# Expert weights dealt to partitions in 8 KB runs, with the down product, the fetch depth and two small pieces rearranged to match

## The chip, the core and the metric

The kernel runs on one core of a Trainium2 chip. The metric is device time in microseconds (us), from the start to the end of one execution, and the number compared is the median over executions.

The engines are named as the profile names them: PE (TensorE, matmuls; PEld is its loading of the stationary operand), ACT (ScalarE), DVE (VectorE), POOL (GpSimd) and SP (SyncE, which issues nearly all weight loads). "SPq L114" and the like is an engine's instruction queue rather than its arithmetic.

## What is computed

Two post-norm layers over 512 tokens of width 1024. Layer 0 mixes the tokens with a state-space model and a pooling branch, layer 1 with stick-breaking attention. After each mixer comes the same feed-forward stage, and only that stage is touched by the change:

```python
for i in range(DEPTH):                       # DEPTH = 2
    ...                                      # the mixer, out projection, layer norm
    ple = (p[i] @ ple_w_proj[i]) * jax.nn.sigmoid(x @ ple_w_gate[i])
    ffn = grouped_moe(x, router_w, router_bias, moe_w1[i], moe_w3[i], moe_w2[i])
    x = layer_norm(DEEPNORM_ALPHA * x + ffn + ple, ...)

def grouped_moe(x, router_w, router_bias, w1, w3, w2):
    ...                                      # sigmoid scores, best group of 4, top 2 experts in it, gates
    h = jax.nn.silu(jnp.einsum('td,edf->etf', xt, w1)) * jnp.einsum('td,edf->etf', xt, w3)
    h = h * gates.T[:, :, None]
    y = jnp.einsum('etf,efd->td', h, w2)
```

There are 16 experts. `w1` and `w3` are 1024 x 512 per expert, `w2` is 512 x 1024, all in fp32, so one expert is 6 MB and one layer's experts are 96 MB.

## The kernel before

`ffn(layer)` writes x to DRAM, routes, and ranks the experts by their number of tokens. It then works through the experts in the order of the table SEQ, which holds ranks: 1, 2, 11, 3, 4, 12, 5, 6, 13, 7, 14, 8, 15, 9, 16, 10. An expert of rank 1 to 10 gets room for 96 tokens (CAP), one of rank 11 to 16 for 64 (SMALL). Tokens beyond that room go through `overflow` (L1141, L1222), an If on all engines that stands behind expert 12 of the order; here it is not entered, but its branch is executed.

For an expert e of the order:

- `gather(e)` (L1015, POOL) fetches its tokens from DRAM into `xg`. `load_g(e)` transposes them on PE (L1042) into a PSUM bank `pT`, from which ACT and DVE make `g`: for a CAP expert a high part on ACT (L87) and a remainder on DVE (L88), for a SMALL one a plain copy.
- `up(e, kh, a)` multiplies `g` with `w1` (a = 0) and `w3` (a = 1), 512 rows (kh) at a time, into the banks `pA`. For CAP each fp32 product is three matmuls (`mm3`, L92 to L94) of high parts and remainders, so the weights too are split: ACT writes `w_..h` (L87), DVE `w_..l` (L88), 1024 columns of a raw tile at a time. For SMALL the raw tile is multiplied directly in fp32 (L1072), two column halves side by side.
- `act(e)` applies silu on ACT (`sg`, L1079 or L1082) and the product on DVE. `turn(e)` transposes `sg` on PE (L1091) and makes `sT`.
- `down(e)` multiplies `sT` with `w2` into the banks `pB` (CAP: `mm3`; SMALL: L1115), ACT evicts to `ysb` (L1139), and `scatter(e)` (L1022, POOL) sends the rows to `yd` in DRAM.

The loop over e interleaves two experts: silu of e, first half of up of e + 1, turn of e, rest of that half, down of e, then `load_g(e + 2)` and the second half of up of e + 1. Behind expert 13 of the order, `last_onehot` (L1198) builds the one-hot matrix of the last expert (`ohl`, 16 small matmuls at L1209 and L1211, evicted by ACT to `oht` and `gs`), so that the last expert's output need not go through DRAM. Behind expert 15 the final sum is made from the reloaded `yd` (`yt`, L1156) and `oht`; one quarter of the gate product (`pG`) and the layer norm follow.

Weights arrive in loads of 1 MB, issued on SP at L114 from a queue planned in advance (`plan_ffn`); six of them belong to an expert. `weights(LA)` and `plain(LA)` take the next raw tile and issue loads up to LA further in the queue. The raw tiles share 17 slots of 8 KB per partition with x, `g`, `xg`, `oht` and others, so a load also waits for a slot. The split halves go through rings of 5 (`wh`) and 6 (`wl`) tiles of 1024 columns. Each engine runs its instructions in the order in which they stand; that order was fixed when the program was built, by a scheduler that models the engines.

The lines that the change touches are the weight load's source view, the operand slices of the transposes, `down`, and the place of `last_onehot`:

```python
src = ap.rearrange("(k p) n -> p k n" if len(ap.shape) == 2 else "o (k p) n -> p (o k) n", p=128)
...
nc.tensor.transpose(p[:, k * c:(k + 1) * c], xgs[:c, e % 2, kb * 128:(kb + 1) * 128],
```

With `(k p)`, a partition of a raw tile holds four separate rows of 512 columns, 2 KB each in DRAM.

## Time and profile before

| | |
|---|---|
| median of 3 executions | 1253.8 us (1252.96 to 1254.33) |
| the profiled execution, its own time | 1255.37 us |
| span of its trace | 1253.7 us |
| PE busy | 1138.2 us (91%) |
| DVE, ACT, POOL busy | 63%, 47%, 10% |
| mean granted TensorE clock | 0.96 |

The profiled execution took 1.57 us more than the median, and its trace leaves 1.67 us of it outside the span; positions below are counted from the span's start. The experts of layer 0 run from about 255 to 549 us, those of layer 1 from about 905 to 1215 us. The page's strip of DMA activity is full in just these stretches; PE is busy nine tenths and more in most of their slices too.

### The profile page before, as it was taken

The numbers are of one execution on the slowest core, as the hardware profiler recorded it, in microseconds if no ns is written. First come the engines' busy times: TensorE is split into PE (matmuls) and PEld (weight loads), VectorE is DVE, ScalarE is ACT, GpSimd is POOL, SyncE is SP. The second block draws the span as 40 slices with busy tenths as digits, with TensorE's granted clock in tenths as the row PEclk, the third lists the DMA queues.
The fourth block names the chain that finished last, engine by engine and source line by source line (L and its number), as shares of the span: only waits on it lengthen the run. The fifth ranks groups of instructions, "written<-read, shape, count | busy, mean of one in ns | idle before, by whom it ended". The sixth has DMA issues, their size and how long they took to land. (4 is left out here: it accounts for less than half of the span.)

```text
span 1253.7 us, 16680 instructions
## 1 busy us (share of the span) xinstructions
PE 1138.2 (91%) x6191; PEld 795.7 (63%) x6191; DVE 790.1 (63%) x1252; ACT 594.4 (47%) x895; POOL 127.8 (10%) x150
## 2 busy tenths in 40 slices
PE   5986998999899887999999999998999899997885
PEld 3866788756457443477867767688865467553454
DVE  5998766866465443486477467756877465443465
ACT  4322542656465443454465456523476465444451
POOL 5010020111010110001000000011101110100001
PEclk9997999999899997999999999998999899988888
DMA  8225563599998996973112024434299999998861
GB/s 248 68 69 189 196 230 114 163 369 375 377 368 298 370 375 245 329 272 101 34 47 89 1 68 151 154 142 153 76 365 370 372 368 322 365 364 291 279 261 67
DMA packets 157391, 285.05 MB, mean 227 GB/s; under 512 B 18816, under 2 KB 42896, under 8 KB 156240
## 3 DMA queue, kind: packets, MB, share of 16 engines
q1 hardware_dynamic: 143760, 256.56, 58.0%
q0 software_dynamic: 8800, 25.19, 6.2%
q10 hardware_dynamic: 4736, 2.10, 0.6%
q8 instruction: 52, 0.85, 0.3%
q14 instruction: 43, 0.35, 0.1%
HBM read 270.45 MB, written 18.61 MB: 231 GB/s over the span
## 5 line engine op out<-in xcount | busy, mean ns | idle before, releaser
L88 DVE TENSOR_TENSOR w_0l<-raw,w_0h 128x1024 fp32r<-128x1024 f32 (+1 forms) x161 | 192.2, 1194 | 72.9 <-ACT w_0h L87 72.1
L87 ACT ACTIVATE w_0h<-raw 128x1024 fp32r<-128x1024 f32 (+1 forms) x161 | 166.4, 1033 | 74.2 <-DMA raw<-in_moe_w_dram 34.7
L88 DVE TENSOR_TENSOR w_2l<-raw,w_2h 128x1024 fp32r<-128x1024 f32 x133 | 162.0, 1218 | 39.8 <-ACT w_2h L87 39.8
L87 ACT ACTIVATE w_2h<-raw 128x1024 fp32r<-128x1024 f32 x133 | 139.7, 1051 | 30.9 <-PE pA L94 28.7
L92 PE MATMUL pA<-w_0h,g 128*96 128x512 f32 x160 | 71.1, 444 | 32.5 <-ACT g L87 28.0
L1072 PE MATMUL pA<-raw,g 128*64 128x512 f32 x384 | 99.6, 621 | 0.0
L1139 ACT ACTIVATE ysb<-pB 96x512 f32<-96x512 f32 (+1 forms) x60 | 35.7, 594 | 97.7 <-PE pB L1115 56.3
L1015 POOL DMA_INDIRECT xg<-xd,ixm x32 | 35.1, 1098 | 363.9 <-PE pT L1042 295.4
L94 PE MATMUL pA<-w_0h,g 128*96 128x512 f32 x160 | 68.0, 425 | 2.1 <-DVE g L88 2.0
L93 PE MATMUL pA<-w_0l,g 128*96 128x512 f32 x160 | 67.9, 424 | 2.2 <-DVE w_0l L88 2.2
L92 PE MATMUL pA<-w_2h,g 128*96 128x512 f32 x160 | 65.9, 412 | 0.0
L93 PE MATMUL pA<-w_2l,g 128*96 128x512 f32 x160 | 65.5, 410 | 0.0
L94 PE MATMUL pA<-w_2h,g 128*96 128x512 f32 x160 | 65.2, 408 | 0.0
L92 PEld LDWEIGHTS pA<-w_0h,g 128*96 128x96 f32 x160 | 27.9, 174 | 56.6 <-ACT g L87 35.1
L1022 POOL DMA_INDIRECT yd<-ysb,ixm x30 | 34.2, 1140 | 241.6 <-ACT ysb L1139 236.7
L1072 PEld LDWEIGHTS pA<-raw,g 128*64 128x64 f32 x384 | 26.1, 139 | 44.1 <-issue 40.1
L692 DVE TENSOR_TENSOR_SCAN kw<-kw 128x128 f32<-128x128 f32 (+3 forms) x64 | 50.2, 812 | 0.9 <-ACT kw L689 0.6
L1115 PE MATMUL pB<-raw,sT 128*64 128x512 f32 x192 | 46.0, 599 | 0.0
L1080 DVE TENSOR_TENSOR sg<-sg,pA 96x512 f32<-96x512 f32 x20 | 13.6, 682 | 47.3 <-PE pA L94 36.6
L1042 PEld LDWEIGHTS pT<-ident,xg 96*128 96x128 f32 (+1 forms) x256 | 22.4, 142 | 28.9 <-issue 20.0
L1042 PE MATMUL pT<-ident,xg 96*128 96x96 f32 (+1 forms) x256 | 26.5, 244 | 15.3 <-DVEq L1222 7.8
L88 DVE TENSOR_TENSOR w_4l<-raw,w_4h 128x1024 fp32r<-128x1024 f32 x20 | 24.4, 1221 | 24.6 <-ACT w_4h L87 24.3
(467 smaller groups left out, 2812.7 us busy)
## 6 DMA issues: line engine op xcount, KB each, us to landing
raw<-in_moe_w_dram SPq DMA_DIRECT2D x192, 1024.0 KB, 11.6
raw<-in_sb_w_qkv_dram SPq DMA_DIRECT2D x12, 1024.0 KB, 5.1
raw<-in_ple_w_gate_dram SPq DMA_DIRECT2D x8, 1024.0 KB, 5.0
yt<-yd SPq DMA_DIRECT2D x8, 1024.0 KB, 8.9
raw<-in_ab_w_out_dram SPq DMA_DIRECT2D x4, 1024.0 KB, 7.7
xd<-x0r POOLq DMA_DIRECT2D x8, 512.0 KB, 4.1
raw<-in_sb_w_out_dram SPq DMA_DIRECT2D x4, 1024.0 KB, 5.4
raw<-in_ab_w_in_dram SPq DMA_DIRECT2D x3, 1024.0 KB
```

The costliest lines, as they stand in the source:

```text
L87: return (self.nc.scalar.activation(hi, src, AF.Copy), (self.nc.gpsimd if pool else self.nc.vector).tensor_tensor(lo, src, hi.bitcast(F32) ...
L88: (self.nc.gpsimd if pool else self.nc.vector).tensor_tensor(lo, src, hi.bitcast(F32), op=OP.subtract))
L92: t.matmul(out, s[0], m[0], start=first, stop=False)
L93: t.matmul(out, s[0], m[1], start=False, stop=False)
L94: t.matmul(out, s[1], m[0], start=False, stop=last)
L692: v.tensor_tensor_scan(rv, rv, rv, 1.0, op0=OP.mult, op1=OP.min)
L1015: return nc.gpsimd.indirect_dma_start(out=xgs[:c, e % 2, :], out_offset=None, in_=xd[:, :], in_offset=bass.IndirectOffsetOnAxis(ap=self.ix ...
L1022: nc.gpsimd.indirect_dma_start(out=yd[:, :], out_offset=bass.IndirectOffsetOnAxis(ap=self.iy[:c, r:r + 1], axis=0), in_=src[:c], in_offset ...
L1042: nc.tensor.transpose(p[:, k * c:(k + 1) * c], xgs[:c, e % 2, kb * 128:(kb + 1) * 128], self.ident[:c, :c])
L1072: nc.tensor.matmul(hh[0][x * 64:x * 64 + 64], g[:, kb], self.pair[x][:, k], start=(kb == 0), stop=(kb == KB - 1))
L1115: nc.tensor.matmul(py[x * 64:x * 64 + 64], sT[:, k], w[x][:, k], start=(k == 0), stop=(k == 3))
L1139: nc.scalar.activation(ysb[:rows(e), h], py, AF.Copy)
```

## The change

Five edits, all in the feed-forward stage or its constants.

1. The expert weights are dealt to partitions by `(p k)` instead of `(k p)`: partition p holds k consecutive rows, one run of 8 KB in DRAM. `w2` is planned as two pieces of 256 rows x 1024 columns instead of two of 512 rows x 512 columns, so that its runs are 8 KB too. The other operand must be dealt in the same way, so the transposes of `xg` read every fourth column of the stationary operand and those of `sg` every second.
2. `down` follows: for CAP both `pB` banks are open at once, one weight piece feeds both column halves, and the two evictions come together at the end. For SMALL the first raw tile is used up before the second.
3. The fetch depth LA stays 6 to the end of the experts instead of falling to 3 at expert 13; a limit keeps the queue from running on into the next layer's weights until the `yt` loads are issued.
4. `last_onehot` stands behind `load_g(e + 2)` instead of ahead of it, and writes its result into the unused end of the last `g` tile instead of a raw slot of its own.
5. The rank constant `kb` is made by GpSimd (an iota and two memsets) instead of three DVE operations.

```diff
     def prefetch(self, upto, parts=1):
-        while self.loaded < min(upto, len(self.queue)):
-            ap, k, n = self.queue[self.loaded]
+        while self.loaded < min(upto, self.limit or len(self.queue)):
+            ap, k, n, rows = self.queue[self.loaded]
...
-            src = ap.rearrange("(k p) n -> p k n" if len(ap.shape) == 2 else "o (k p) n -> p (o k) n", p=128)
+            o = "" if len(ap.shape) == 2 else "o "
+            src = ap.rearrange(f"{o}(p k) n -> p ({o}k) n" if rows else f"{o}(k p) n -> p ({o}k) n", p=128)
...
-        nc.vector.tensor_copy(self.kb, self.w16)
+        nc.gpsimd.iota(self.kb, pattern=[[-1, 16]], base=16, channel_multiplier=0,
+                       allow_small_or_imprecise_dtypes=True)
         for e in range(2):
-            nc.vector.tensor_scalar(self.kb[:, e:e + 1], self.kb[:, e:e + 1], float((2 - e) << 15), None, op0=OP.add)
+            nc.gpsimd.memset(self.kb[:, e:e + 1], float(((2 - e) << 15) + 16 - e))
...
-                    kb = hf * 4 + k
-                    nc.tensor.transpose(p[:, k * c:(k + 1) * c], xgs[:c, e % 2, kb * 128:(kb + 1) * 128],
+                    nc.tensor.transpose(p[:, k * c:(k + 1) * c], xgs[:c, e % 2, hf * 512 + k:(hf + 1) * 512:4],
...
-                nc.tensor.transpose(p[:, k * c:(k + 1) * c], sg[:, k * 128:(k + 1) * 128], self.ident[:c, :c])
+                a = k // 2 * 256
+                nc.tensor.transpose(p[:, k * c:(k + 1) * c], sg[:, a + k % 2:a + 256:2], self.ident[:c, :c])
...
             if rows(e) == CAP:
-                for h in hs:
+                py = [self.bank("B", "pB")[:CAP] for _ in hs]
+                for a in range(2):
                     w = self.weights(LA)
-                    py = self.bank("B", "pB")[:CAP]
-                    for k in range(4):
-                        self.mm3(py, (sT[:, 0, k], sT[:, 1, k]), w[k], k == 0, k == 3)
-                    yield h, py
-                return
-            w = [self.plain(LA), self.plain(LA)]
...
+                    for q in range(2):
+                        k = 2 * a + q
+                        for x, h in enumerate(hs):
+                            self.mm3(py[x], (sT[:, 0, k], sT[:, 1, k]), [t[:, h] for t in w[q]], k == 0, k == 3)
...
+            yield from zip(hs, py)
+
+        self.limit = self.ends[layer]
...
-            LA = 6 if e < 13 else 3
...
-            if e == NE - 3:
-                oht = self.last_onehot()
-                self.ln_setup("ln_ffn", layer)
...
             if e + 2 < NE:
                 gn = load_g(e + 2)
+            if e == NE - 3:
+                oht = self.last_onehot(self.gtile[:, 2 * KB * CAP:])
+                self.ln_setup("ln_ffn", layer)
...
+        self.limit = None
+        LA = 3
...
-                self.plan(part(e, n, slice(kh * 512, (kh + 1) * 512)), 4, 512)
+                self.plan(part(e, n, slice(kh * 512, (kh + 1) * 512)), 4, 512, True)
...
-                self.plan(part(e, "moe_w2", slice(None), slice(nh * 512, (nh + 1) * 512)), 4, 512)
+                self.plan(part(e, "moe_w2", slice(nh * 256, (nh + 1) * 256)), 2, 1024, True)
...
+        self.ends[layer] = len(self.queue)
```

The program is scheduled anew, so instructions also move where the diff shows nothing. Three places matter. The line numbers of the changed kernel are a few higher (L87 is L89 there, L92 to L94 are L94 to L96, L1072 is L1076, L1139 is L1147); `raw_1722` and the like are raw tiles by number, and `w_0h` and `w_2h` (or `w_1h`) are the two halves of one raw tile after ACT's split.

The first place is ACT around the end of the first CAP expert's down product in layer 0. Before:

```order
L87 ACTIVATE w_0h<-raw_1722 128x1024
L87 ACTIVATE w_2h<-raw_1722 128x1024
L1139 ACTIVATE ysb<-pB 96x512
L87 ACTIVATE w_0h<-raw_2150 128x1024
L87 ACTIVATE w_2h<-raw_2150 128x1024
L1139 ACTIVATE ysb<-pB 96x512
L1051 ACTIVATE g_2_2284<-pT 128x256
```

and after the change:

```order
L89 ACTIVATE w_0h<-raw_1722 128x1024
L89 ACTIVATE w_2h<-raw_1722 128x1024
L89 ACTIVATE w_0h<-raw_2150 128x1024
L89 ACTIVATE w_2h<-raw_2150 128x1024
L1147 ACTIVATE ysb<-pB 96x512 x2
L1055 ACTIVATE g_2_2284<-pT 128x256
```

The first eviction has moved behind the two splits for the next expert, and both now stand together. What follows them is the same.

The second place is ACT near the end of layer 0's experts, from the evictions of expert 13 of the order on (`g_15` belongs to the last expert, a CAP one; `sg` with 64 rows and `ysb` with 64 rows to expert 14, a SMALL one). Before:

```order
L1139 ACTIVATE ysb<-pB 96x512 x2
L1213 ACTIVATE oht<-pT 128x512
L1215 ACTIVATE gs<-pT 128x1
L87 ACTIVATE g_15_4584<-pT 128x384 x2
L87 ACTIVATE w_0h<-raw_4521 128x1024
L87 ACTIVATE w_2h<-raw_4521 128x1024
L1082 ACT_TABLE_LOAD
L1082 ACTIVATE sg<-pA 64x512
L87 ACTIVATE w_0h<-raw_4599 128x1024
L87 ACTIVATE w_2h<-raw_4599 128x1024
L1139 ACTIVATE ysb<-pB 64x512 x2
L87 ACTIVATE w_0h<-raw_4645 128x1024
```

and after the change:

```order
L1147 ACTIVATE ysb<-pB 96x512 x2
L89 ACTIVATE w_0h<-raw_4482 128x1024
L1086 ACT_TABLE_LOAD
L1086 ACTIVATE sg<-pA 64x512
L89 ACTIVATE w_2h<-raw_4482 128x1024
L89 ACTIVATE w_0h<-raw_4484 128x1024
L89 ACTIVATE w_2h<-raw_4484 128x1024
L89 ACTIVATE g_15_4554<-pT 128x384 x2
L1222 ACTIVATE g_15_4554<-pT 128x512
L1224 ACTIVATE gs<-pT 128x1
L89 ACTIVATE w_0h<-raw_4604 128x1024
L89 ACTIVATE w_2h<-raw_4604 128x1024
```

The last expert's `g_15` has moved behind the silu of expert 14 and three weight splits. The splits of its second half of w1 and w3 (`raw_4604` here, `raw_4645` before) have moved ahead of the evictions of expert 14.

The third place is PE at the same point, where `ohl` is the one-hot matrix of `last_onehot`. Before, from the end of expert 13's down product:

```order
L94 MATMUL pB<-w_2h,sT 96x512
L1209 MATMUL pT<-ident,ohl 128x128 x8
L1211 MATMUL pT<-gates_1776,ohl 128x1 x8
L1072 MATMUL pA<-raw_4431,g_14_4418 64x512
L1042 MATMUL pT<-ident,xg_1500 128x96 x8
L1072 MATMUL pA<-raw_4453,g_14_4418 64x512
```

and after the change, from the end of expert 14's second up half:

```order
L1076 MATMUL pA<-raw_4431,g_14_4418 64x512
L1076 MATMUL pA<-raw_4453,g_14_4418 64x512
L94 MATMUL pA<-w_0h,g_15_4554 96x512
L95 MATMUL pA<-w_0l,g_15_4554 96x512
L94 MATMUL pA<-w_0h,g_15_4554 96x512
L1219 MATMUL pT<-ident,ohl 128x128 x8
L1221 MATMUL pT<-gates_1776,ohl 128x1 x8
L96 MATMUL pA<-w_0h,g_15_4554 96x512
```

The one-hot matmuls have moved behind expert 14's up product and behind the first three matmuls of expert 15. Further on, six matmuls of the gate (`pG`) now stand between the transposes of expert 15's `sg` and the rest of its down product, where before the whole of `pG` came behind it.

## Rows read from the trace of the kernel before

**Rows 1.** The page's first part: busy time, share of the span, instructions.
```profile
PE 1138.2 (91%) x6191; PEld 795.7 (63%) x6191; DVE 790.1 (63%) x1252; ACT 594.4 (47%) x895; POOL 127.8 (10%) x150
```

**Rows 2.** Windows: length; busy PE, PEld, DVE, ACT, POOL; clock; DMA share; GB/s.
```profile
255.00:485.00 230.00, 214.48 (x1014) 125.81 (x1013) 126.49 (x137) 119.40 (x154) 27.23 (x24) 0.96 1.01 360
885.00:1190.00 305.00, 282.26 (x1383) 173.25 (x1382) 174.77 (x228) 160.04 (x202) 35.99 (x33) 0.96 0.92 324
265.00:270.00 5.00, 5.00 (x21) 2.70 (x21) 1.78 (x2) 1.68 (x3) 0.00 (x0) 1.00 1.05 388
540.00:545.00 5.00, 3.86 (x13) 2.32 (x14) 4.65 (x6) 3.81 (x8) 0.00 (x0) 0.75 1.01 424
1205.00:1210.00 5.00, 3.58 (x17) 1.92 (x15) 4.10 (x4) 3.94 (x6) 0.00 (x0) 1.00 1.03 431
```

**Rows 3.** The page's DMA issues: count, KB each, median us to landing.
```profile
raw<-in_moe_w_dram SPq DMA_DIRECT2D x192, 1024.0 KB, 11.6
```

**Rows 4.** What PE waited for, 230 to 560 us: total us, times, longest.
```profile
PE pA L92 <- ACT g L87: 14.0, 5, 5.0
PE pT L1042 <- DVEq L1222: 3.7, 1, 3.7
PE pT L1042 <- PEq L1222: 2.5, 1, 2.5
PE pA L92 <- ACT w_0h L87: 2.2, 1, 2.2
```

**Rows 5.** What ACT waited for in the same stretch, the row on loads.
```profile
ACT w_0h L87 <- DMA raw<-in_moe_w_dram: 15.0, 8, 4.3
```

**Rows 6.** ACT's timeline: start, length, instruction, idle before and releaser.
```profile
325.77 0.59 ACT L1082 ACTIVATE sg<-pA 64x512 f32<-64x512 f32 x1 [3.69 <-PE pA L1072]
326.38 1.06 ACT L87 ACTIVATE w_0h<-raw 128x1024 fp32r<-128x1024 f32 x1
...
330.18 0.85 ACT L87 ACTIVATE g<-pT 128x384 fp32r<-128x384 f32 x2
```

**Rows 7.** PE's timeline at the same place.
```profile
330.70 0.62 PE L92 MATMUL pA<-w_0h,g 128*96 128x512 f32 x1 [5.01 <-ACT g L87]
...
336.69 0.63 PE L94 MATMUL pA<-w_2h,g 128*96 128x512 f32 x1
```

**Rows 8.** ACT's timeline near the end of layer 0's experts.
```profile
518.28 0.59 ACT L1082 ACTIVATE sg<-pA 64x512 f32<-64x512 f32 x1
...
529.17 1.20 ACT L1139 ACTIVATE ysb<-pB 64x512 f32<-64x512 f32 x2 [8.26 <-PE pB L1115]
```

**Rows 9.** PE's timeline there, experts 13 to 15 of the order.
```profile
501.56 1.94 PE L1072 MATMUL pA<-raw,g 128*64 128x512 f32 x8
503.43 0.47 PE L92 MATMUL pB<-w_0h,sT 128*96 128x512 f32 x1
...
509.06 1.95 PE L1209 MATMUL pT<-ident,ohl 128*128 128x128 f32 x16
...
512.62 1.07 PE L1072 MATMUL pA<-raw,g 128*64 128x512 f32 x2
...
531.36 0.47 PE L92 MATMUL pA<-w_0h,g 128*96 128x512 f32 x1 [2.23 <-ACT w_0h L87]
532.62 0.74 PE L93 MATMUL pA<-w_0l,g 128*96 128x512 f32 x1 [0.79 <-DVE w_0l L88]
...
540.35 0.55 PE L1091 MATMUL pT<-ident,sg 96*128 96x96 f32 x4 [0.78 <-DVE sg L1080]
541.48 0.47 PE L92 MATMUL pB<-w_0h,sT 128*96 128x512 f32 x1 [0.58 <-ACT sT L87]
...
549.09 0.28 PE L92 MATMUL pG<-w_0h,cath 128*128 128x256 f32 x1
```

**Rows 10.** Stationary loads by line: ns min/median/max, first and last start, form.
```profile
L286 PEld LDWEIGHTS pT<-ident,s5in x16: 183/202/205, 25.1 to 29.8; 64*128 64x128 f32 x16
L181 PEld LDWEIGHTS pT<-ident,x x32: 180/230/231, 7.7 to 24.5; 128*128 128x128 f32 x32
```

More of the change, by code (lines that the diff above doesn't have):

```diff
@@ L55, in __init__ @@
         self.cat = None
+        self.limit = None
+        self.ends = {}
         self.order = {}
@@ L94, in mm3, with plan @@
         t.matmul(out, s[1], m[0], start=False, stop=last)
-    def plan(self, ap, k, n):
-        self.queue.append((ap, k, n))
+    def plan(self, ap, k, n, rows=False):
+        self.queue.append((ap, k, n, rows))
         return len(self.queue) - 1
     def prefetch(self, upto, parts=1):
-        while self.loaded < min(upto, len(self.queue)):
-            ap, k, n = self.queue[self.loaded]
+        while self.loaded < min(upto, self.limit or len(self.queue)):
+            ap, k, n, rows = self.queue[self.loaded]
             if callable(ap):
@@ L121, in weights @@
         self.used += 1
-        ap, k, n = self.queue[i]
+        _, k, n, _ = self.queue[i]
         raw = self.raws.pop(i)
@@ L490, in plain @@
         self.used += 1
-        ap, k, n = self.queue[i]
+        _, k, n, _ = self.queue[i]
         return self.raws.pop(i)[:, :k * n].rearrange("p (k n) -> p k n", k=k)
@@ L1034, in load_g @@
             if c == CAP:
-                g = self.slot(f"g{layer}_{e}", F32R)[:, :2 * KB * c].rearrange("p (a k t) -> p a k t", a=2, k=KB)
+                self.gtile = self.slot(f"g{layer}_{e}", F32R)
+                g = self.gtile[:, :2 * KB * c].rearrange("p (a k t) -> p a k t", a=2, k=KB)
             else:
@@ L1157, in ffn @@
             yts.append(yt)
+        self.limit = None
+        LA = 3
         yl = self.slot(f"yl{layer}", F32R).rearrange("p (a d) -> p a d", a=2)
@@ L1196, in ffn, with last_onehot @@
             pass
-    def last_onehot(self):
+    def last_onehot(self, oht):
         nc, v = self.nc, self.nc.vector
@@ L1211, in last_onehot @@
             nc.tensor.matmul(pg[:, 0:1], oh[:, x], self.gates[:, x % 2, x // 2], start=(x == 0), stop=(x == 2 * NT - 1))
-        oht = self.slot("oht", F32R)[:, :512]
         nc.scalar.activation(oht, p, AF.Copy)
```

15 lines of the change are left out of this document (9 added, 6 removed).

## The prediction

> **What bounds the kernel now.** I read the page's busy shares first, then the windows over the two expert stretches, then what PE waited for in them, and last the timelines around the longest waits. PE is busy 91% of the span [rows 1]. In the expert stretches it is busy 214.5 us of 230 and 282.3 of 305, while the DMA engines are busy all of the time or nearly so (shares of 1.01 and 0.92) [rows 2]. So two resources look full, and the first question is which of them holds the end. The waits answer it: in layer 0's expert stage PE waits 14.0 us for `g` from ACT, 6.2 us at the overflow branch and 2.2 us for a split weight [rows 4]; no row of that list names a transfer of expert weights as what PE waited for. ACT does wait for weight loads, 15.0 us in 8 places [rows 5], but PE isn't held there, since the splits run ahead of it. So PE, with the order in which ACT serves it, is the bound, and DMA is a close second with little to spare.
>
> What PE's longest wait looks like: ACT sits idle until a SMALL expert's up product is done, then runs silu (0.59 us), four weight splits and only then the `g` that PE needs; from 326.38 to 330.18 are four splits, 0.95 us each [rows 6]. PE waits 5.01 us there, and its next 13 CAP matmuls (330.70 to 336.69, a short second wait among them) take 5.99 us where 13 at the pace of expert 13's down product, 24 in 5.63 us or 0.235 each [rows 7, 9], would take 3.05. Without the second wait (about half a us) that is some 2.4 us lost to a lower granted clock after the wait. That it is the clock I take from the window 540 to 545, just behind two shorter waits: its mean granted clock is 0.75, while those without a wait ahead of them show 1.00 [rows 2]. A wait of several us therefore costs about half as much again.
>
> **The change part by part.**
>
> *8 KB runs.* The same 192 loads of 1 MB [rows 3] move the same bytes. In stretches where weight loads alone run, with 2 KB pieces, 388 GB/s were reached; in those where the `yt` loads with their 8 KB rows ran in the queue 424 and 431 [rows 2]. 1.049 MB take 2.70 us at 388 GB/s and 2.45 at the mean of the latter two, 0.25 us less; for 192 loads 48 us of DMA time. Little of it is on the path: where ACT waits less for a load, it then waits longer for PE. I take 0; the bounds are 0 and the rival below.
>
> *Strided operands of the transposes.* The same number of transposes, with a stationary operand read at a stride of 16 or 8 bytes. The nearest row is L286, which reads every sixteenth fp32 column: 183 to 205 ns a load; L181 in the same early stage, unit stride, takes 180 to 231 [rows 10]. The shapes differ (64 partitions against 128), and stride shows no price. I take 0, with the rival below as upper end.
> The Trainium skill speaks against it: "SBUF — State Buffer", in Door 1: The DMA port swizzle, states that SBUF has 16-byte lines, needs two hits on a line for full bandwidth and lets an access that crosses to a new one pay. By it the stride of 16 bytes here would pay at each element, as should the one of 64 bytes in L286; the trace does not agree [rows 10]. By the row the sum has nothing for this edit; by the rule it would have the price of the last rival.
>
> *The new down.* The matmul count is the same. In the ACT order one eviction moves behind two splits. That lets ACT split the next expert's weights up to half a down product (2.8 us) sooner, but what PE waits for next is `g` or `sT` behind the same instructions as before, so I take 0. The scatter starts up to 0.6 us later, and nobody on PE waits for it.
>
> *Fetch depth, and `last_onehot`.* They act only behind expert 13, where the order is a different one. Layer 0, from PE's rows [rows 9] and ACT's [rows 8]:
> - Removed: PE waits 2.23 us for the first split of expert 15's second half, which stood behind an eviction that waited 8.26 us for PE; it now stands ahead. From there to the wait before 540.35 the 24 matmuls take 540.35 - 0.78 - 531.36 = 8.21 us against 5.63: 2.58 more, of which 0.79 is a second wait and the rest the lower clock. The wait of 0.58 for `sT` is filled with six gate matmuls. The down product then takes 549.09 - 541.48 = 7.61 us against 5.63, 1.98 more. Together 2.23 + 2.58 + 0.58 + 1.98 = 7.4 us.
> - Added: `g_15` now stands behind expert 14's silu and three splits. ACT can start that silu only when PE ends expert 14's up product; with the one-hot matmuls (512.62 - 509.06 = 3.56 us) moved behind, that is near 513.4. The table load ahead of the silu fits into ACT's idle time. Then 0.59 + 3 x 0.95 + 0.43 (half of the 0.85 for `g`) = 3.9 us, so PE waits about 4.0 us, as in [rows 7], and loses about 2.4 us of clock after it. The one-hot matmuls, now behind three of expert 15's, also need both `pT` banks back from `g`'s remainder on DVE: about 0.5 us. Together 6.9 us.
> - Between them stands an amount that I can't place. The stretch is 549.09 - 509.06 = 40.0 us long. In it are 72 CAP matmuls (16.9 us), the one-hot ones (3.6), 32 records of SMALL products (four times the 1.87 us that eight take from 501.56), sixteen transposes (about 2.2, from the four of 0.55 at 540.35), waits of 2.23 + 0.79 + 0.78 + 0.58 = 4.4 and clock losses of 1.8 + 2.0: 38.4 in all. The other 1.6 us lie where single SMALL products stand among other work, an estimate. The new order has them in groups of four and eight, so part of it goes.
>
> Net of the tail: between 7.4 - 6.9 = 0.5 us and 0.5 + 1.6 + 2.4 = 4.5 us saved, the latter if the clock doesn't fall after the new wait. At the other end, if the lower clock in the down product stays (the wait of 0.78 for `sg` is still ahead of it) and the wait for `g_15` is 5.0 as in [rows 7]: 0.5 - 2.0 - 1.0 = -2.5, a loss. I take 2.0 us saved in each layer, between the first two, since most of what is removed stands in rows and the dearer form of the new wait doesn't. Layer 1 has the same order. That `oht` no longer takes a slot only matters to loads that PE doesn't wait for.
>
> *Rank constant.* Three DVE operations at the start become three on POOL, which is busy a tenth of the span [rows 1]; nothing of the experts starts before the router needs it. 0. If POOL were late there, it would be by the length of such an operation, below what can be seen.
>
> *The rest.* The overflow branch keeps its 6.2 us per layer: they are waits for the sequencers, which the change doesn't touch. The long waits for `g`, 14.0 us per layer, stay too: their order on ACT (silu, two or four splits, then `g`) is the same.
>
> Sum: the profiled execution's 1255.4 us less 2 x 2.0 = 4.0 us gives 1251.4; that execution stands 1.6 above the median. On the median's scale 1253.8 - 4.0 = **1249.8 us**.
>
> **The rivals.**
>
> *DMA was the bound after all.* For it: shares of 1.01 and 0.92, ACT's 15.0 us of waiting for loads [rows 2, 5]. Then faster loads would shorten the experts until PE is full. PE's free time in the two stretches is 15.5 + 22.7 = 38.2 us [rows 2], less than the 48 us of DMA time, so it would be 1253.8 - 38.2 = 1215.6, about 1216. Against it: nothing in [rows 4] names a load, and the largest of those waits begin with ACT waiting for PE [rows 6].
>
> *Nothing measurable.* The tail's new wait eats what the old ones gave (0.5 us saved per layer, the lower end above), or the scheduler's new order does nothing elsewhere: 1253.8 - 1.0 = 1252.8.
>
> *Slower, through `g_15`.* In the tail PE waits for `g_15` behind expert 14's silu and three splits. With 5.0 us of wait, the clock loss behind it, and the down product still at the lower clock, each layer loses 2.5 us, so 1253.8 + 5.0 = 1258.8. It decides from the point where the new wait with its clock exceeds 7.4 us. For it: three waits of this very form stand in the experts and cost 14.0 us per layer with shorter ones [rows 4]. Against it: here are three splits, not four.
>
> *Slower, through the strides.* Each of the 384 transposes would take the length of a load such as those of [rows 10], some 0.2 us, once more, if PE can't hide it: 384 x 0.2 = 77 us, 1331. The same rows speak against it.
> By the cited rule of the Trainium skill's SBUF page it would be this case.
>
> **How the numbers follow.** Chances: the forecast (1244.8 to 1252.3) 0.53, DMA bound 0.13, nothing 0.15, slower through `g_15` 0.17, strides 0.02. A change of 0.2%, 2.5 us, is about what a measurement of this kernel can tell from none. Of the forecast's 0.53 some 0.1 lies within that, so faster is 0.43 + 0.13 = 0.56, within 0.1 + 0.15 = 0.25, slower 0.17 + 0.02 = 0.19. The range takes in the tail's bounds on the slow side (1253.8 + 5.0, rounded up to 1260). On the fast side it goes to 1226, some way towards the DMA rival, because part of ACT's waits for loads could turn out to reach PE. Left out are most of that rival and the strides, and a little above 1260, together under 0.2.
>
> **What would show it.** Right: weight loads land sooner and the DMA share in the expert stretches falls to about 0.9; the waits for `g` at the three places of [rows 4] are unchanged; the wait of 2.2 us for `w_0h` near the end of the experts is gone, and one of about 4 us for `g` stands some 15 us earlier; the transposes' stationary loads keep their mean. Wrong: PE's waits for `g` in mid stage shrink, the loads of L1042's successor take longer, or the expert stage as a whole is shorter by ten us or more, which would mean that ACT's waits for loads did reach PE.

## The result, and the profile after the change

The changed kernel takes 1267.3 us (median of 4 executions, 1262.87 to 1272.53), the kernel before 1253.6 (4 executions): a ratio of 1.011 with a 95% interval of 1.006 to 1.016. It is slower by 13.7 us where 4 us less were forecast, and outside the forecast range. The profiled execution took 1270.5 us, with a span of 1268.7.

The page looks almost the same. Its first part, which answers to [rows 1]:

```profile
PE 1155.3 (91%) x6191; PEld 819.9 (65%) x6191; DVE 790.2 (62%) x1249; ACT 595.3 (47%) x895; POOL 129.7 (10%) x153
```

PE has the same 6191 matmuls and is busy 17.1 us longer: PE itself does its work more slowly. The DMA side got what it was meant to get. The windows of the changed kernel (columns as in [rows 2]) and its DMA issues:

```profile
255.00:490.00 235.00, 218.74 (x1002) 131.15 (x1002) 125.25 (x136) 117.66 (x150) 27.75 (x24) 0.96 0.91 348
265.00:270.00 5.00, 5.00 (x22) 2.97 (x20) 2.77 (x3) 1.73 (x2) 0.00 (x0) 1.00 1.01 419
```

```profile
raw<-in_moe_w_dram SPq DMA_DIRECT2D x192, 1024.0 KB, 8.3
```

In the same five microseconds 419 GB/s where there were 388, a DMA share of 0.91 in the expert stretch where there was 1.01, and 8.3 us from issue to landing instead of 11.6 [rows 3]. And the kernel is slower.

To see where, I took the start of PE's first transpose of `xg` for each expert, of its down products and of the final sum from the two traces, and set the stretches between them side by side (us, from the profiled executions; experts of the order are counted from 0, so expert 13 is the last but two, and the third expert is number 2):

| stretch on PE | before | after | difference |
|---|---|---|---|
| start to the first expert, layer 0 | 228.8 | 225.2 | -3.6 |
| first to third expert | 26.6 | 28.7 | +2.1 |
| third expert to expert 13 of the order | 205.9 | 213.0 | +7.1 |
| to expert 13's down product (branch in it) | 42.1 | 41.8 | -0.3 |
| to expert 15's down product | 38.1 | 42.7 | +4.6 |
| to the final sum | 14.8 | 12.7 | -2.1 |
| to the first expert of layer 1 | 339.5 | 340.0 | +0.5 |
| first to third expert, layer 1 | 26.5 | 27.3 | +0.8 |
| third expert to expert 13 | 206.5 | 213.4 | +6.9 |
| to expert 13's down product (branch in it) | 40.9 | 37.1 | -3.8 |
| to expert 15's down product | 39.3 | 42.5 | +3.2 |
| to the final sum, and to the end | 44.7 | 44.3 | -0.4 |

Four things stand in it: mid stage is 7 us longer in each layer, the tail some 2.5 us (4.6 less 2.1, and 3.2 less 0.4), and two stretches are shorter in places that the prediction passed over, the start and the branch of layer 1.

**Mid stage.** The groups of stationary loads, one line per shape (busy us, mean ns of one, then idle time before them), of the kernel before:

```profile
L1042 PEld LDWEIGHTS pT<-ident,xg 96*128 96x128 f32 x160 | 15.0, 141 | 9.8 <-issue 6.4 <-ACT gs L1215 1.6
L1091 PEld LDWEIGHTS pT<-ident,sg 96*128 96x128 f32 x80 | 8.1, 144 | 14.6 <-DVE g L1049 4.9 <-issue 4.7 <-DVE sg L1080 4.1
```

and of the changed kernel, where L1046 and L1096 are the same transposes with strided columns:

```profile
L1046 PEld LDWEIGHTS pT<-ident,xg 96*128 96x128 f32 x160 | 22.3, 216 | 8.1 <-issue 6.5
L1096 PEld LDWEIGHTS pT<-ident,sg 96*128 96x128 f32 x80 | 11.6, 212 | 14.3 <-DVE g L1053 4.9 <-issue 4.5 <-DVE sg L1084 4.3
```

Each load takes some 70 ns longer, with a stride of two columns as with one of four. There are 384 of them, so some 27 us more of loading; the transposes' own matmul records grew from 43.3 us in all to 59.1. That is most of PE's 17 us.

**The tail.** PE's timeline of the changed kernel, experts 14 and 15 of layer 0:

```profile
523.02 0.47 PE L94 MATMUL pA<-w_0h,g 128*96 128x512 f32 x1 [4.06 <-ACT g L89]
...
524.96 3.75 PE L1219 MATMUL pT<-ident,ohl 128*128 128x128 f32 x16 [0.82 <-DVE g L90]
528.50 3.41 PE L1221 MATMUL pT<-gates,ohl 128*128 128x1 f32 x16
531.78 0.72 PE L96 MATMUL pA<-w_0h,g 128*96 128x512 f32 x1
...
536.94 0.60 PE L95 MATMUL pA<-w_0l,g 128*96 128x512 f32 x1
```

The wait for the last `g` is there with 4.06 us (4.0 were forecast). What was not forecast is what the one-hot matmuls cost behind it: they take 531.78 - 524.96 = 6.8 us where they took 3.56 [rows 9]. The window over them shows why:

```profile
525.00:537.00 12.00, 12.00 (x47) 9.98 (x47) 0.28 (x1) 3.40 (x5) 0.00 (x0) 0.50 0.86 338
```

The granted clock is 0.50, the lower of the two levels (1.2 GHz), for all of these twelve microseconds, in which PE is never idle; in the window behind, 537 to 549, it is 0.99.

**The start.** DVE's and PE's timeline of the kernel before:

```profile
12.67 0.17 DVE L167 COPY kb<-w 128x16 f32<-128x16 f32 x1 [7.08 <-POOL w L164]
...
13.01 0.21 DVE L247 COPY s5sm<-pT 128x64 f32<-128x64 f32 x1
```

```profile
13.51 1.11 PE L181 MATMUL pT<-ident,x 128*128 128x128 f32 x4 [4.64 <-ACT s5sm L248]
```

DVE's copy of the rank constant waited 7.08 us for GpSimd's iota, and everything behind it on DVE's queue waited with it, up to a PSUM bank that PE needed. In the changed kernel the copy of `s5sm` stands at 5.63 us and PE goes on at 9.51 with a wait of 0.78:

```profile
5.63 0.17 DVE L251 COPY s5sm<-pT 128x64 f32<-128x64 f32 x1
```

```profile
9.51 1.97 PE L185 MATMUL pT<-ident,x 128*128 128x128 f32 x8 [0.78 <-ACT s5sm L252]
```

**The branch.** PE's waits over the whole run, the rows for DVE's overflow branch, first of before, then of after:

```profile
PE pT L1042 <- DVEq L1222: 7.8, 2, 4.2
```

```profile
PE pT L1046 <- DVEq L1231: 2.9, 1, 2.9
```

In layer 1 the wait is gone.

### The profile page after: what moved, and what is told of

It is laid out like the page before. It is cut to its first block, busy times and chain, and to the rows that moved or that the text cites. A ratio compares the mean times of both kernels' runs of the same rounds, so it can differ in the third digit from the quotient of the medians.

```text
span 1268.7 us, 16688 instructions
## 1 busy us (share of the span) xinstructions
PE 1155.3 (91%) x6191; PEld 819.9 (65%) x6191; DVE 790.2 (62%) x1249; ACT 595.3 (47%) x895; POOL 129.7 (10%) x153
## 5 line engine op out<-in xcount | busy, mean ns | idle before, releaser
L89 ACT ACTIVATE w_0h<-raw 128x1024 fp32r<-128x1024 f32 (+1 forms) x161 | 166.4, 1033 | 49.7 <-PE pG L96 27.2
L90 DVE TENSOR_TENSOR w_2l<-raw,w_2h 128x1024 fp32r<-128x1024 f32 x93 | 113.4, 1220 | 47.7 <-ACT w_2h L89 47.6
L89 ACT ACTIVATE w_2h<-raw 128x1024 fp32r<-128x1024 f32 x93 | 97.9, 1053 | 48.2 <-PE pA L96 40.7
L94 PE MATMUL pA<-w_0h,g 128*96 128x512 f32 x160 | 71.5, 447 | 35.4 <-ACT g L89 35.4
L1076 PE MATMUL pA<-raw,g 128*64 128x512 f32 x384 | 97.3, 620 | 0.0
L1147 ACT ACTIVATE ysb<-pB 96x512 f32<-96x512 f32 (+1 forms) x60 | 35.3, 591 | 105.2 <-PE pB L1124 58.8
L96 PE MATMUL pA<-w_0h,g 128*96 128x512 f32 x160 | 68.3, 427 | 2.0 <-DVE g L90 1.9
L94 PEld LDWEIGHTS pA<-w_0h,g 128*96 128x96 f32 x160 | 28.3, 177 | 59.1 <-ACT g L89 44.3
L94 PE MATMUL pA<-w_2h,g 128*96 128x512 f32 x160 | 65.9, 412 | 0.0
L96 PE MATMUL pA<-w_2h,g 128*96 128x512 f32 x160 | 65.3, 408 | 0.0
L1076 PEld LDWEIGHTS pA<-raw,g 128*64 128x64 f32 x384 | 25.8, 139 | 43.5 <-issue 39.9
L90 DVE TENSOR_TENSOR w_1l<-raw,w_1h 128x1024 fp32r<-128x1024 f32 x40 | 48.8, 1219 | 3.6 <-ACT w_1h L89 3.2
L1046 PEld LDWEIGHTS pT<-ident,xg 96*128 96x128 f32 (+1 forms) x256 | 34.8, 215 | 22.5 <-issue 15.0
L89 ACT ACTIVATE w_1h<-raw 128x1024 fp32r<-128x1024 f32 x40 | 42.0, 1051 | 10.6 <-PE pA L96 10.6
L1046 PE MATMUL pT<-ident,xg 96*128 96x96 f32 (+1 forms) x256 | 37.0, 285 | 10.7 <-PEq L1231 5.0
L1084 DVE TENSOR_TENSOR sg<-sg,pA 96x512 f32<-96x512 f32 x20 | 13.6, 682 | 48.6 <-PE pA L96 48.6
```

Source lines behind the costliest of these rows:

```text
L89: return (self.nc.scalar.activation(hi, src, AF.Copy), (self.nc.gpsimd if pool else self.nc.vector).tensor_tensor(lo, src, hi.bitcast(F32) ...
L90: (self.nc.gpsimd if pool else self.nc.vector).tensor_tensor(lo, src, hi.bitcast(F32), op=OP.subtract))
L94: t.matmul(out, s[0], m[0], start=first, stop=False)
L96: t.matmul(out, s[1], m[0], start=False, stop=last)
L1076: nc.tensor.matmul(hh[0][x * 64:x * 64 + 64], g[:, kb], self.pair[x][:, k], start=(kb == 0), stop=(kb == KB - 1))
L1084: v.tensor_tensor(sg, sg, hh[1][:CAP], op=OP.mult)
```

## The experiments

Theories: S, the strided loads are the main cost; T, the new tail; D, something on the DMA side. Later ones are named where they come up. Medians stand beside the kernel before measured in the same session, with the ratio's 95% interval.

**e1: the changed kernel with unit-stride reads.** PE, ACT and SP have the same instructions in the same order as in the changed kernel.

```diff
-                    nc.tensor.transpose(p[:, k * c:(k + 1) * c], xgs[:c, e % 2, hf * 512 + k:(hf + 1) * 512:4],
+                    nc.tensor.transpose(p[:, k * c:(k + 1) * c], xgs[:c, e % 2, hf * 512 + k * 128:hf * 512 + (k + 1) * 128],
...
-                nc.tensor.transpose(p[:, k * c:(k + 1) * c], sg[:, a + k % 2:a + 256:2], self.ident[:c, :c])
+                nc.tensor.transpose(p[:, k * c:(k + 1) * c], sg[:, k * 128:(k + 1) * 128], self.ident[:c, :c])
```

> The changed kernel with the transposes of xg and sg reading unit-stride columns again; the instruction order is the same on every engine. Which features meet which weight rows is then wrong: this leaves out the dealing of the other operand, the work is the same. Theory S (the strided stationary loads cost time on PE: 213 ns a load in the changed kernel against 142 before, PE busy 59.1 us on the 384 transposes against 43.3): some 14 to 16 us less than the changed kernel, about 1252, and loads of about 142 ns. Theory D (the strides are hidden and something of the larger DMA runs or the tail holds the kernel): no change, about 1267. Theory T (the tail's new order is the main cost): still about 1262 or more.

1252.9 us (10 executions), before 1253.4, ratio 1.000 (0.999 to 1.001). So the strides are worth 14.5 us, as theory S had it, and without them the change would be a draw. The changed kernel's four executions lie up to 10 us apart, so a difference from it is known to some 6 us only; e2 and e3 give the strides' price again. The draw is itself a sum, as the next runs show.

**e2: the kernel before with strided reads alone.**

```diff
-                    nc.tensor.transpose(p[:, k * c:(k + 1) * c], xgs[:c, e % 2, kb * 128:(kb + 1) * 128],
+                    nc.tensor.transpose(p[:, k * c:(k + 1) * c], xgs[:c, e % 2, hf * 512 + k:(hf + 1) * 512:4],
...
-                nc.tensor.transpose(p[:, k * c:(k + 1) * c], sg[:, k * 128:(k + 1) * 128], self.ident[:c, :c])
+                nc.tensor.transpose(p[:, k * c:(k + 1) * c], sg[:, k // 2 * 256 + k % 2:k // 2 * 256 + 256:2], self.ident[:c, :c])
```

> The kernel before, with strided reads in the transposes alone (every fourth column of xg, every second of sg); the order is the same as before on every engine, weights as before, so the dealing of features to rows is wrong. Theory S: about 1253.6 + 14 = 1268. Theory D and T: about 1254, since nothing else moved.

1273.0 us against 1253.4, ratio 1.016 (1.014 to 1.019): 19.5 us for the strides here. A third pair is e3 and e6 below, which differ in the strides alone: 1267.1 less 1250.8, 16.3 us. The spread of the changed kernel's executions covers the difference between the three.

**e3: the changed kernel with the old tail**, edits 3 and 4 undone.

```diff
-        self.limit = self.ends[layer]
...
+            LA = 6 if e < 13 else 3
...
+            if e == NE - 3:
+                oht = self.last_onehot(self.slot("oht", F32R)[:, :512])
+                self.ln_setup("ln_ffn", layer)
             if e in GATES:
                 gate(GATES.index(e))
...
-            if e == NE - 3:
-                oht = self.last_onehot(self.gtile[:, 2 * KB * CAP:])
-                self.ln_setup("ln_ffn", layer)
```

> The changed kernel with the fetch depth and the place and slot of the last one-hot as before (edits 3 and 4 undone). The last g then stands ahead of the silu on ACT again. Theory T: the wait of 4 us for the last g with the slow one-hot matmuls behind it goes, 3 to 5 us a layer, about 1258 to 1261. Theory S with a neutral tail: 1266 to 1268.

1267.1 us, where the changed kernel has 1267.3: theory T gets nothing from this pair, though the spread of the changed kernel's executions could hide a few us.

**e4: the kernel before with the new tail alone**, the same edits the other way round.

> The kernel before with edits 3 and 4 alone (fetch depth, place and slot of the last one-hot). Theory T: 3 to 5 us a layer slower, about 1260. Theory S with a neutral tail: 1252 to 1255.

1259.3 us against 1253.4, ratio 1.005 (1.003 to 1.007), 5.8 us slower. Its tail reads like that of the changed kernel: a wait of 4.07 us for the last `g`, then the one-hot matmuls from 519.15, the next group of them at 522.69. So T holds on the old kernel, and whether it holds on the new one e3 alone can't tell; e6 and e13 below say more.

**e5: the kernel before with the rank constant on GpSimd**, edit 5 alone.

```diff
-        nc.vector.tensor_copy(self.kb, self.w16)
+        nc.gpsimd.iota(self.kb, pattern=[[-1, 16]], base=16, channel_multiplier=0,
+                       allow_small_or_imprecise_dtypes=True)
         for e in range(2):
-            nc.vector.tensor_scalar(self.kb[:, e:e + 1], self.kb[:, e:e + 1], float((2 - e) << 15), None, op0=OP.add)
+            nc.gpsimd.memset(self.kb[:, e:e + 1], float(((2 - e) << 15) + 16 - e))
```

> The kernel before with edit 5 alone (rank constant on GpSimd). Theory K: in the trace of before DVE stands 7.08 us at the copy of the rank constant, waiting for GpSimd's iota, with work behind it for which PE waits 4.6 us; that goes, 4 to 5 us. The same edit takes three instructions off DVE's program; the wait for DVE's branch in layer 1, 4.2 us, is absent in the three runs that have this edit and present in the three that don't, so it may go too: 1245 to 1249. The view of my prediction (a constant that nothing waits for): 1253.

1244.0 us against 1252.9, ratio 0.993 (0.991 to 0.995). The smallest edit is worth 8.9 us, more than was expected of it, and alone it beats both kernels. Its trace has the first expert at 225.0 us instead of 228.8, and the branch row of layer 1 is gone:

```profile
PE pT L1043 <- DVEq L1223: 3.1, 1, 3.1
```

**e6: the changed kernel with unit reads and the old tail.** What is left of the change is the 8 KB runs, the new down product and the rank constant (the edits of e1 and e3 together).

> The changed kernel with unit-stride reads in the transposes (so that features meet the wrong weight rows, the work being the same) and with edits 3 and 4 undone: it keeps the 8 KB runs, the new down product and the rank constant. If the costs add up, e1's 1252.9 less the 5 us that the new tail cost in e4: about 1247 to 1248. If the tail is neutral in this layout, as the pair of the changed kernel and e3 seemed to say: about 1253.

1250.8 us (10 executions) against 1252.9, ratio 0.998 (0.997 to 0.999). Between the two expectations: the tail costs 2.1 us here (e1's 1252.9 less 1250.8), not 5.8.

**e7: as e6, in short runs.** The instructions of PE, ACT, DVE and GpSimd are the same in the same order; only the loads' source views differ.

```diff
-                self.plan(part(e, n, slice(kh * 512, (kh + 1) * 512)), 4, 512, True)
+                self.plan(part(e, n, slice(kh * 512, (kh + 1) * 512)), 4, 512)
...
-                self.plan(part(e, "moe_w2", slice(nh * 256, (nh + 1) * 256)), 2, 1024, True)
+                self.plan(part(e, "moe_w2", slice(nh * 256, (nh + 1) * 256)), 2, 1024)
```

> As e6, but with the weights dealt by (k p) again, in runs of 2 KB for w1 and w3 and of 4 KB for w2. PE, ACT, DVE and GpSimd have the same instructions in the same order as e6, so the pair tells what the run length itself is worth. Theory B (PE and ACT's order are the bound, the run length is worth nothing): within 2 us of e6. Theory D (DMA a second bound): 4 us or more slower than e6. With unit reads and (k p) the features meet the right rows.

1250.0 us (10 executions), where e6 has 1250.8: the 8 KB runs are worth nothing. What ACT waited for loads, over the whole run, in before, in e7 and in e6:

```profile
ACT w_0h L87 <- DMA raw<-in_moe_w_dram: 34.7, 19, 6.2
```

```profile
ACT w_0h L89 <- DMA raw<-in_moe_w_dram: 16.8, 10, 2.6
```

```profile
ACT w_0h L89 <- DMA raw<-in_moe_w_dram: 3.2, 4, 1.5
```

From e7 to e6 13.6 us of ACT's waiting go, and no time with them. The loads land in 8.8 us in e6 and 9.9 in e7, so the run length by itself is about a third of the 3.3 us by which they land sooner in the changed kernel than before. And e7 less e5, 6.0 us, is the price of the new down product with its cut of `w2`, which had been put at nothing. The stretch from the final sum of layer 0 to the first expert of layer 1 is 343.2 us in e7 and 339.4 in e5. ACT's timelines there, e5 and then e7:

```profile
541.24 0.67 ACT L1161 ACTIVATE yl<-pB,gs 96x512 fp32r<-96x512 f32 x1
543.00 0.69 ACT L1161 ACTIVATE yl<-pB,gs 96x512 fp32r<-96x512 f32 x1 [1.10 <-PE pB L94]
543.71 1.28 ACT L979 ACT_TABLE_LOAD   x1
548.75 0.60 ACT L979 ACTIVATE sg<-pG 128x512 f32<-128x512 f32 x1 [3.77 <-PE pG L94]
```

```profile
544.24 1.28 ACT L982 ACT_TABLE_LOAD   x1
552.01 0.60 ACT L982 ACTIVATE sg<-pG 128x512 f32<-128x512 f32 x1 [6.49 <-PE pG L96]
552.51 1.25 ACT L1168 ACTIVATE yl<-pB,gs 96x512 fp32r<-96x512 f32 x2
```

In e5 the last expert's output is evicted as each half is done and ACT then waits for the gate's product. In e7 both evictions come at the end, and the scheduler put the sigmoid ahead of them: they stand behind its wait of 6.49 us, and with them the final sum and the layer norm. That was a reading; e13 tests it. It concerns the new down with the old tail: with the new tail, in the changed kernel and in e1, ACT's evictions (L1170) stand ahead of the sigmoid (in e1 at 547.69 against 553.40).

**e8: the columns dealt where they are written.** An attempt to keep the 8 KB runs without strided loads: GpSimd copies x into the dealt order before it goes to DRAM, and ACT and DVE write `sg` in the dealt order; the transposes read unit stride. Old tail.

```diff
+            xp = self.half4("xp")
+            nc.gpsimd.tensor_copy(xp.rearrange("p (h k j) -> p h k j", h=2, k=4),
+                                  xt[i].rearrange("p (h j k) -> p h j k", h=2, k=4))
-            nc.gpsimd.dma_start(xd[i * 128:(i + 1) * 128, :], xt[i])
+            nc.gpsimd.dma_start(xd[i * 128:(i + 1) * 128, :], xp)
...
-                nc.scalar.activation(sg, hh[0][:CAP], AF.Silu)
-                v.tensor_tensor(sg, sg, hh[1][:CAP], op=OP.mult)
+                nc.scalar.activation(lin(sg), dealt(hh[0][:CAP]), AF.Silu)
+                v.tensor_tensor(lin(sg), lin(sg), dealt(hh[1][:CAP]), op=OP.mult)
```

> The changed kernel with the columns dealt where they are written instead of where PE reads them: GpSimd copies x into the dealt order before it goes to DRAM, ACT and DVE write sg in the dealt order out of PSUM; the transposes read unit stride. Fetch depth and last one-hot as before. If the dealing is free there: as e6, about 1248. If GpSimd's copies hold the gather of the first expert, or the strided reads of PSUM slow silu and its product ahead of the turn: each of 15 turns a layer by some tenths of a us, up to 1256.

1263.8 us against 1252.9, ratio 1.008 (1.006 to 1.010), above both expectations. The expert stretches are within 2 us of those of e6 (206.8 and 207.0 us from the third expert to expert 13, against 208.4 and 206.4), so writing `sg` dealt costs no time there, though DVE is busy some 13 us longer over the whole run than in e6. The first expert comes 5.5 us later in each layer, behind GpSimd's copies of 2.5 us each (that they are what delays it is inferred from the place), and the wait for DVE's branch is back in layer 1.

**e9: a probe of the stride.** The kernel before; `xg` is read in steps of eight columns, `sg` at unit stride, and L286, on which the prediction had rested, at unit stride.

```diff
-                    nc.tensor.transpose(p[:, k * c:(k + 1) * c], xgs[:c, e % 2, kb * 128:(kb + 1) * 128],
+                    nc.tensor.transpose(p[:, k * c:(k + 1) * c], xgs[:c, e % 2, kb::8],
...
-                nc.tensor.transpose(p[:, h].rearrange("p v g -> p (v g)"), self.bsl[:64, x * 8 + h::16],
+                nc.tensor.transpose(p[:, h].rearrange("p v g -> p (v g)"), self.bsl[:64, (x * 8 + h) * 128:(x * 8 + h + 1) * 128],
```

> A probe on the kernel before with two reads changed, so that features are misplaced but the work is the same: the transposes of xg read every eighth column (steps of 32 bytes), those of sg stay at unit stride; and L286, whose row with steps of 64 bytes I had taken as the sign that a stride is free, reads unit stride. Theory R (a strided load takes some 200 ns whatever the step and the clock, a unit one 140 at the full clock and more at the low clock): the loads of xg take about 215 ns as with steps of 16 bytes, and L286 without its stride takes 200 to 230 like the unit-stride L181 in that stage, so its row could not show a price. Rival (the price grows with the step): over 250 ns for xg. Rival (L286 did show a free stride): L286 unchanged within 5 ns. Time about 1253 + 10 = 1263.

Its loads, and L286 (min, median, max):

```profile
L1042 PEld LDWEIGHTS pT<-ident,xg 96*128 96x128 f32 x160 | 20.3, 203 | 9.2 <-issue 6.4 <-ACT gs L1215 1.6
L1091 PEld LDWEIGHTS pT<-ident,sg 96*128 96x128 f32 x80 | 7.8, 141 | 14.8 <-DVE g L1049 4.9 <-issue 4.8 <-DVE sg L1080 4.1
```

```profile
L286 PEld LDWEIGHTS pT<-ident,s5in x16: 179/221/221, 25.1 to 29.7; 64*128 64x128 f32 x16
```

Steps of eight columns cost 203 ns, no more than steps of two or four. And L286 takes 221 ns at unit stride where it took 202 with a stride of sixteen [rows 10]: in that early stage a unit-stride load is no faster than a strided one, so its row could show no price. 1263.7 us against 1253.3 (2 executions): 10.4 us for the 256 transposes of `xg`.

**e10 and e11: the two tail edits apart**, each on e5: e10 the fetch depth (edit 3), e11 the last one-hot (edit 4).

> e5 (before with the rank constant on GpSimd) and edit 3 alone: fetch depth 6 to the end. In ACT's order the last g then stands behind the silu and four splits, as in e4. Theory T3 (the depth lets weights be split first and so pushes the last g back): 2 to 6 us above e5, 1246 to 1250. If it is the place of the last one-hot instead: as e5, 1244.

> e5 and edit 4 alone: the last one-hot behind the last g, its result in the g tile. In ACT's order the last g then stands ahead of the silu and even ahead of the second eviction. Theory T3: as e5 or up to 2 us below, 1242 to 1244. If the place of the one-hot matmuls is what costs: 2 to 6 us above e5.

1245.1 and 1246.0 us, e5 being 1244.0 in an earlier session; before was 1253.3 here and 1252.9 there, so by ratios 0.9935 and 0.994 against 0.993, with overlapping intervals. Neither edit costs 2 us by itself beyond doubt; theory T3 doesn't hold as I put it. In e10 the last `g` is behind the silu, as in e4, but the one-hot matmuls stand ahead of it and run at full pace:

```profile
503.78 1.95 PE L1214 MATMUL pT<-ident,ohl 128*128 128x128 f32 x16
505.56 1.84 PE L1216 MATMUL pT<-gates,ohl 128*128 128x1 f32 x16
```

PE waits there all the same, 3.19 us ahead of the last `g`'s transposes, but 512-column matmuls follow those, not the one-hot ones. It takes both edits to put the one-hot matmuls behind a wait of 4 us, where they run at the lower clock.

**e12: e5 with three idle DVE instructions near the start**, to bring the number ahead of the branch back to what it was.

```diff
+        pad = cp.tile([128, 1], F32, name="pad")
+        for e in range(3):
+            nc.vector.memset(pad, float(e))
```

> e5 with three tiny DVE instructions (memsets of one column that nothing reads) added near the start, so that DVE's program has as many instructions ahead of the overflow branch as before. Theory P (the wait of 4.2 us for DVE's branch in layer 1 went in e5 because the program behind it moved by three instructions): the wait is back, about 1248. Rival (it went for another reason, such as the time at which the branch is reached): as e5, 1244.

1248.4 us (7 executions) against 1253.3, ratio 0.996 (0.995 to 0.997), 4.5 above e5 by the medians of two sessions and 4.0 by the ratios, and the wait is back:

```profile
PE pT L1046 <- DVEq L1226: 6.8, 2, 3.7
```

So of e5's 8.9 us about half is this: three instructions fewer on DVE ahead of the branch. The rival falls. What sets it beyond the count is open: e8 has as many DVE instructions as e7, in another order, and has the wait.

**e13: e7 with the last expert's down product as before.**

```diff
+            if e == NE - 1:
+                for h in hs:
+                    w = self.weights(LA)
+                    py = self.bank("B", "pB")[:CAP]
+                    for k in range(4):
+                        self.mm3(py, (sT[:, 0, k], sT[:, 1, k]), w[k], k == 0, k == 3)
+                    yield h, py
+                return
...
+                if e == NE - 1:
+                    self.plan(part(e, "moe_w2", slice(None), slice(nh * 512, (nh + 1) * 512)), 4, 512)
```

> e7 (unit reads, short runs, old tail, rank constant on GpSimd, new down) with the down product of the last expert alone as before (one column half after the other, each evicted when it is done). In e7 ACT evicts the last expert's two halves behind the gate's sigmoid, in e5 ahead of it; here ahead of it again. Theory Y (that order is why the stretch from the last product to the next layer's first expert is 343.2 us in e7 against 339.4 in e5): 3 to 4 us below e7, about 1246, and the stretch back at about 339.5. Rival (the stretch is longer for another reason, or the new down costs elsewhere): within 1 us of e7, 1250.

1247.1 us against 1254.8, ratio 0.994 (0.992 to 0.996), where e7 had 0.9975: the expected 3 to 4 us. The stretch is 338.0 us, and ACT's evictions stand ahead of the sigmoid again, at 543.52 and 545.31. This also explains why the new tail costs less in e1 against e6 than in e4: by the two traces the tails themselves are 2.4 and 2.9 us longer, but the new tail moves the last evictions back ahead of the sigmoid, and the stretch falls from 343.0 to 340.1. The same happens from e3 to the changed kernel (342.2 to 340.0), which gives back some 2 us there; the rest of that pair's missing cost isn't explained and lies within the spread.

**The sum**, from differences of medians:

| step | from | us |
|---|---|---|
| rank constant on GpSimd | e5 less before | -8.9 |
| new down product, `w2` cut by rows | e7 less e5 | +6.0 |
| 8 KB runs | e6 less e7 | +0.8 |
| fetch depth and last one-hot | e1 less e6 | +2.1 |
| strided transposes | after less e1 | +14.5 |
| together | | +14.5 |

The measured difference is 13.7; 14.5 is the changed kernel against e5's session of the kernel before. The steps add up because each starts where the last one ends, so the total checks nothing. And their order matters: the tail is worth 2.1 us behind the new down and 5.8 ahead of it (e4). If e4, e5 and e1 add, the new down with its 8 KB runs is worth only 1252.9 - (1253.4 - 8.9 + 5.8) = 2.6 us behind the tail, an estimate; the two together are worth some 8 us, and how they share it is a matter of order. Of the new down's 6.0 us in e7, e13 gives back 3 to 4; some 3 us stand in layer 0's mid stage (208.4 us against 205.3 from the third expert to expert 13), with one more wait of 0.87 us for a weight's remainder among them. Where the rest of those comes from stays open.

## Why the prediction was wrong

**The bound: right.** PE with ACT's order holds the end. DMA, with a share of 1.01, was no bound: e6 and e7 differ by 0.8 us, and the rival of 1216 us is ruled out. The waits of [rows 4] for `g` stayed: 28.0 us in ten places over both layers in e5, e6 and e11, as before; the changed kernel has 35.4 in twelve, two of them new ones in the tails.

**Strided operands at nothing: wrong, 14.5 us, the step that decided.** The forecast took L286 against L181 [rows 10], rows of the first 30 us, for a price in the experts. There unit-stride loads take 220 to 230 ns; in the experts they take 141 to 150 in the same trace, and L181 itself, later in the kernel before, has a median of 141:

```profile
L181 PEld LDWEIGHTS pT<-ident,x0r x96: 138/141/231, 183.3 to 869.8; 128*128 128x128 f32 x96
```

A strided load takes 200 to 217 in either stage (202 for L286). So the comparison came from a stage in which every load is slow. PE's timeline of the kernel before shows what is different there:

```profile
32.82 0.63 PE L93 MATMUL pA<-x0Tl,w_4h 128*128 128x512 f32 x1
33.25 0.63 PE L94 MATMUL pA<-x0Th,w_4l 128*128 128x512 f32 x1
...
34.50 0.39 PE L92 MATMUL pA<-x0Th,w_4h 128*128 128x512 f32 x1
34.73 0.39 PE L93 MATMUL pA<-x0Tl,w_4h 128*128 128x512 f32 x1
```

Up to 33.7 us the 512-column matmuls start 0.43 us apart, as they do in the changed kernel's tail at a granted clock of 0.50 (532.30 to 535.71 there), and from 34.5 on 0.23 apart. The views print a clock of 1.00 for the early stretch, but the trace has no clock record before 33.9 us. The experts agree: the few unit-stride loads that fall into stretches at 0.50 take as long as those at the start (the four of `xg` from 496.5 us in the kernel before: median 221 ns), and strided ones are no slower there (the four from 501.8 us in the changed kernel: 215). So at the lower level these strides show no price; at the full one, where nearly all of the experts' loads run, they cost 70 ns. The prediction had named the sign itself: "the loads of L1042's successor take longer". The rival had the right cause and a price five times too high, 77 us: it took a whole load again for each transpose, where the load grew by 70 ns and, by the three pairs, half to three quarters of that showed as time.

The Trainium skill's rule in "SBUF — State Buffer", Door 1: The DMA port swizzle, spoke for that cost, and the prediction let the row from the other stage overrule it. It was right that these strides cost. That two hits on a 16-byte line are enough is not what the runs show: steps of 8 bytes put two elements on a line, and their loads take 208 to 212 ns against 144 to 150, like those of 16 and 32 bytes.

**Rank constant at nothing: wrong, by 8.9 us to the other side.** The reason given was that nothing needs the constant before the router. But an instruction on an in-order queue delays what stands behind it. The wait of 7.08 us was in DVE's timeline of the kernel before; the prediction has no row of DVE's queue from the first 20 us. That accounts for some 4 us; another 4 to 4.5, the branch, could not have been read from the trace of before, and "The overflow branch keeps its 6.2 us per layer" was wrong for layer 1.

**New down at nothing: wrong, by 6.0 us with the old tail (e7), by some 2 to 3 with the new one.** The forecast asked what PE waits for in mid stage and did not follow ACT's order at the end of the layer, where the last down's evictions feed the final sum: `yl` and the sigmoid of the gate change places in e7. In the changed kernel they don't, so that part isn't in its time. The longer mid stage of layer 0 is; the prediction put that at nothing too, and its cause is open.

**Tail at -2.0 us per layer: wrong sign, +2.5 us per layer in the trace.** The wait was sized right (4.06 us against 4.0), and so was most of what it replaced. The mis-sized term is the clock behind it: 2.4 us were put in, as after a wait that dense 512-column matmuls follow. Here the one-hot matmuls follow, at the lower level from start to end: 3.3 us more for them, and the ten CAP matmuls from 531.78 lose some 2 us all the same, together 5.3 us.

**8 KB runs at nothing: right**, for the reason given.

## What to carry to other kernels

Compare a price only with rows from the same stage, and see first at which pace the engine runs in it: a load that is slow for everybody at the start says nothing about a stage in which unit stride is fast. A printed clock is worth no more than the matmuls' own spacing beside it. Before costing an edit at nothing, look at what stands behind each touched instruction on its queue, in the first microseconds and the last as well as in the stage that the edit is meant for. A transfer that nobody on the critical engine waits for gives nothing when it gets faster, and a layout that makes it faster is paid for wherever the other operand is read.

## What the runs showed of the hardware

- A stationary load of 128 fp32 columns takes 141 to 150 ns at unit stride in the experts and 200 to 217 at steps of 2, 4 and 8 columns; the price doesn't grow with the step. Where matmuls run at the pace of the lower clock level, unit-stride loads take about 221 to 230 too (L286 in e9, L181 up to 24.5 us, four loads at 496.5 us), and the stride has no price.
- 32 small matmuls behind a wait of 4 us ran at a granted clock of 0.50, with PE busy all the time, in 6.8 us; ahead of that wait they take 3.6. The ten 512-column matmuls behind them ran at the lower level too, and those from 537 on at the full one.
- Three idle DVE instructions near the start are worth 4 to 4.5 us at a branch more than 1100 us later: DVE's wait behind it in layer 1 comes and goes with them. The count alone doesn't decide it: e8 has the wait with the lower count.
- With nothing else changed, weight loads of 1 MB landed in 8.8 us in runs of 8 KB (e6) and in 9.9 in runs of 2 and 4 KB (e7); with PE's order as the bound, that was worth nothing.
